# A Macaron block with one Strassen-Winograd level: the quads' merge regrouped, one output half accumulated upon a sum in PSUM

## The chip, the cores and the metric

One core of one Trainium2 chip runs the whole block. The metric is the device time of one execution in microseconds, as the median of several runs. The program is also run once under the hardware profiler, which gives each engine's instructions with their start and length.

## The reference

A Macaron block of width 2048 on 256 tokens: a SwiGLU feed-forward network (FFN) of inner width 5632, a mixer (an RWKV-7 branch and a pooling branch), and a second FFN. All inputs are float32.

```python
D_MODEL = 2048
SEQ = 256
D_FF = 5632

def _swiglu(x, w_gate, w_up, w_down):
    return (jax.nn.silu(x @ w_gate) * (x @ w_up)) @ w_down
...
        f = _swiglu(_rmsnorm(h, ln_ffn1_pre[l]), ffn1_gate[l], ffn1_up[l], ffn1_down[l])
        h = h + MACARON_WEIGHT * _rmsnorm(f, ln_ffn1_post[l])
...
        h = h + _rmsnorm(mx, ln_mix_post[l])
        f = _swiglu(_rmsnorm(h, ln_ffn2_pre[l]), ffn2_gate[l], ffn2_up[l], ffn2_down[l])
        h = h + MACARON_WEIGHT * _rmsnorm(f, ln_ffn2_post[l])
```

## The kernel before

**Products.** A float32 product is made of three matmuls (`mm3`, L317): each operand is split into a rounded high part and a low part, and high by high, high by low and low by high are added up in a PSUM bank. The low and high parts of a weight tile are made on the fly: ScalarE (ACT) casts the tile (`wH`), VectorE (DVE) subtracts the cast from the tile (`wL`, called a *low* here), TensorE (PE) multiplies. The pairs `wH`, `wL` lie in a ring of five buffers (`WS_BUFS`), so a cast waits until PE has used the tile five entries back.

**Blocks.** `seven` (L508) computes two output column blocks of 512 at once: `f` (first) and `l` (last), each for the two halves of the tokens (0 and 1), in four PSUM banks f0, f1, l0, l1. In an FFN's gate and up stage a block is 512 columns of gate (`f`) and the same of up (`l`), with 16 tiles of the inner dimension; there are blocks 0 to 10, and blocks 2 to 10 use this function with quads. Blocks 0 and 1 have none. In the down stage two calls make four column blocks of the output; the second has a *trail* of 16 inner tiles that are multiplied half by half after all else, the first half of the tokens first (`by_half`).

**Orders.** What PE does in a block is written out in a string. `f` or `l` is a *pair*: two inner tiles by one column block, both halves, 12 matmuls. `q` is a *quad*: two inner tiles by both column blocks and both halves, done with seven products in place of eight (one Strassen-Winograd level), 21 matmuls where two pairs take 24. A quad needs sums of the activations (`sums`), made once per stage, and sums of the weight tiles (t13, two halves of t24), made on DVE for every quad, as well as seven lows in four instructions. Four of its products go to banks of their own (p1, p5, p6, p7), the others into f0, l0 and l1.

**Merge.** After the last quad of a block, `merge` adds the four p banks up: ACT copies p1 into u0, then DVE makes u1 = p6 + u0, u2 = p7 + u1, u1 = p5 + u1, u3 = p5 + u2 (L645). DVE adds f0 to u1 and f1 to u3 when the pairs of `f` are done (also L645), and l0 to u0 and l1 to u2 when the block is done (`total`, L693). That is eight additions of 512 columns. ACT applies silu to the gate half, DVE multiplies (`mult`, L1074) and transposes in 32-by-32 blocks (`turn`, L875).

**What sets the order.** PE follows the strings. The order on DVE, ACT and the queues comes from a planner (`Plan.solve`) that gives each operation a due time, counted back from the PE step that needs it, and places the operations with fixed costs. It sets an order only: at run time each engine works through its list and waits on semaphores.

**Ends.** After the trail, `end` (L1185) squares the last column block, adds up, takes the power -1/2 on GpSimd (POOL), scales and writes out. In the FFNs the squares are summed by a DVE instruction (L1173); in the mixer's output stage, where `direct` is true, by ACT (L987).

Of the kernel before, what the change touches and what calls it, by code (L numbers as in the profile page):

```python
# [13 lines left out]
ALU = mybir.AluOpType  # L14
# [33 lines left out]
GATE_UP = ["", "ffffffffllllllll"] + ["ffqfqfqlqlll", "fffqffqlqllll", "ffqfqfqlqlll", "fffqffqlqllll", "ffqfqfqlqlll", "fffqffqlqllll", "ffqfqfqlqlll", "fffqffqlqllll", "ffqfqfqlqlll"]  # L48
# [172 lines left out]
class Block:  # L221
# [95 lines left out]
    def mm3(s, ps, aH, aL, bH, bL, start, stop):  # L317
        nc = s.nc
        nc.tensor.matmul(ps, aH, bH, start=start, stop=False)  # L319
        nc.tensor.matmul(ps, aH, bL, start=False, stop=False)  # L320
        nc.tensor.matmul(ps, aL, bH, start=False, stop=stop)  # L321
# [99 lines left out]
    def sums(s, T, Td, j, out, own=None, nq=2, used=(), x32=None):  # L421
# [13 lines left out]
        def second():  # L435
# [72 lines left out]
    def seven(s, wf, cf, wl, cl, at, dep, KT, need, sm, order, ev_f, ev_l, used, trail=0):  # L508
# [9 lines left out]
        left = dict(f0=std + n, f1=std, l0=std + n, l1=std + n, p1=n, p5=n, p6=n, p7=n)  # L518
# [9 lines left out]
        def mul(b, x, wt):  # L528
            left[b] -= 1
            new = b not in bank  # L530
            if new:
                bank[b] = s.psum("ms") if b[0] == "p" else s.pm.tile(
                    [P, 512], F32, tag="mm", name=s.nm("mm"))
            s.mm3(bank[b], *x, *wt, new, left[b] == 0)
# [9 lines left out]
        def pair(k, w, c0, b, by_dma):  # L544
            low, dst = s.fetch(w, k, c0, keep, by_dma, by_dma)

            def do():
                for i in range(2):
                    for h in range(2):
                        mul(f"{b}{h}", rows(k + i, h), ws[k + i])  # L550
            d = p.pe(12 * MM, do, [low, dep(k)] + claim(b + "0", b + "1"), dst)
# [3 lines left out]
        def quad(q):  # L555
# [10 lines left out]
            def get(m):  # L566
# [3 lines left out]
                w, c0 = ((wl, cl), (wf, cf))[(m + i) % 2]  # L570
# [32 lines left out]
            def half(n_, m, deps, rel):  # L603
# [15 lines left out]
                                  mul("f0", S_(4), x["a"][1])),  # L619
                 [la, ds, dep(k)] + claim("p1", "f0", "f1"), ra)  # L620
            p.pe(3 * MM, lambda: mul("l0", rows(k + 1, 0), x["b"][0]),
                 [lb] + claim("l0", "l1"), rb)
# [4 lines left out]
                                      mul("l1", rows(k + 1, 1), x["t24"][1])),  # L627
# [14 lines left out]
        def add(o, b, i):  # L642
            if u[o] is None:
                new(o)
            V.tensor_tensor(out=u[o], in0=bank[b], in1=u[i], op=ALU.add)  # L645
        m, use = {}, {}

        def merge(d):
            for i in range(4):
                use[i] = p.claim("tmp")  # L650
# [3 lines left out]
            for o, b, i in ((1, "p6", 0), (2, "p7", 1), (1, "p5", 1), (3, "p5", 2)):  # L654
                d = m[f"u{o}"] = p.op("DVE", one, lambda o=o, b=b, i=i: add(o, b, i),
                                      [d] + (use[o][0] if o > 1 or b == "p6" else []))
                held[b].append(d)
                use[i][1].append(d)
        nq, last = 0, {}
        ks = dict(f=iter(range(K0, KT, 2)), l=iter(range(K0, KT - trail, 2)))  # L660
        for c in order:
# [12 lines left out]
            if c == "f" and left["f"] == std // 2:  # L674
                m["f"] = last["f"]

                def close_f():
                    for h, i in ((0, 1), (1, 3)):
                        if n:
                            d = p.op("DVE", one, lambda h=h, i=i: add(i, f"f{h}", i),  # L680
                                     [last["f"], m[f"u{i}"], last["q"]])
# [5 lines left out]
                if not n or "u3" in m:  # L687
# [4 lines left out]
        def total(h):  # L692
            V.tensor_tensor(out=u[2 * h], in0=bank[f"l{h}"], in1=u[2 * h], op=ALU.add)  # L693
# [1321 lines left out]
```

## Time and profile before

| what | value |
|---|---|
| median of 3 runs | 2017.59 us (2016.92 to 2018.37) |
| the profiled execution's span | 2015.4 us |
| PE busy | 2000.9 us |
| DVE busy | 1824.7 us |
| ACT busy | 1192.3 us |
| granted TensorE clock, mean | 0.998 |

The profiled execution has no time of its own beside the span, which runs from its first to its last instruction; the timed runs contain about 2.2 us more (2017.59 less 2015.4), the start and the end around it. Busy shares over the whole span mix stages: the mixer lies between about 700 and 1340 us, the first FFN before and the second behind it.

### The profile page before, as it was taken

Reading aid. Unit: us, or ns where it says so; the run is one execution under the profiler, and the core shown is the slowest. Engines: PE = TensorE matmul, PEld = TensorE weight load, DVE = VectorE, ACT = ScalarE, POOL = GpSimd, SP = SyncE. Lnnn points to the kernel's source line nnn. Section 1 sums busy time; section 2 is a strip of 40 time slices with the busy share of each in tenths; the row PEclk is TensorE's granted clock in tenths of the full one; section 3 lists DMA queues with packets and bytes.
Section 4 is the critical chain, followed back from the end, with each engine's and each line's share of the span. In section 5 each row is a group of like instructions: output and inputs, shape, how many; then the busy total and the mean of one; then the engine's idle time right before and its main releaser. Section 6 shows DMA issues by size and latency. Waiting matters only on the chain.

```text
span 2015.4 us, 28684 instructions
## 1 busy us (share of the span) xinstructions
PE 2000.9 (99%) x9957; PEld 1655.1 (82%) x9957; DVE 1824.7 (91%) x2424; ACT 1192.3 (59%) x1586; POOL 327.6 (16%) x673
## 2 busy tenths in 40 slices
PE   9999999999999999999999999999999999999997
PEld 7888888888888888888788788888888888888886
DVE  6999999999999957789689678979999999999997
ACT  7555665556666566685476434665656555566663
POOL 0111211131000123403220111011113111310000
PEclk9999999999999999999999999999999999999999
DMA  7675674667568577757456547666656747665683
GB/s 268 224 241 182 220 242 160 218 213 241 175 203 299 209 212 214 205 175 214 146 173 190 159 168 269 244 216 215 228 198 218 245 142 235 211 228 183 207 294 126
DMA packets 227419, 423.56 MB, mean 210 GB/s; under 512 B 24639, under 2 KB 28105, under 8 KB 227273
## 3 DMA queue, kind: packets, MB, share of 16 engines
q1 hardware_dynamic: 204713, 384.70, 57.9%
q0 software_dynamic: 22272, 36.51, 5.5%
q8 instruction: 78, 1.28, 0.3%
q10 hardware_dynamic: 288, 0.52, 0.1%
q14 instruction: 68, 0.56, 0.1%
HBM read 396.69 MB, written 8.39 MB: 201 GB/s over the span
## 4 chain that ended last, share of the span: by engine, by line
PE 97%; DVE 1%; issue 1%; DMA 0%; ACT 0%; POOLq 0%; POOL 0%; DVEq 0%; ACTq 0%
PE mm L319 27%; PE mm L321 26%; PE mm L320 26%; PE ms L320 5%; PE ms L321 5%; PE ms L319 5%; PE tr L849 1%; PE pA L1733 0%; DVE u L645 0%; PE mc L817 0%; DMA x<-in_x_dram 0%; PE pU L1829 0%; PE pSa L1841 0%; PE pY L1864 0%; PE pT L1900 0%
## 5 line engine op out<-in xcount | busy, mean ns | idle before, releaser
L319 PE MATMUL mm<-wH,xH 128*128 128x512 f32 (+1 forms) x2116 | 825.5, 391 | 0.0
L320 PE MATMUL mm<-wL,xH 128*128 128x512 f32 (+1 forms) x2116 | 821.2, 388 | 0.0
L321 PE MATMUL mm<-wH,xL 128*128 128x512 f32 (+1 forms) x2116 | 821.1, 388 | 0.0
L319 PEld LDWEIGHTS mm<-wH,xH 128*128 128x128 f32 x2116 | 397.4, 188 | 82.1
L321 PEld LDWEIGHTS mm<-wH,xL 128*128 128x128 f32 x2116 | 397.4, 188 | 82.0 <-DVE xL L867 0.2
L373 ACT CAST wH<-w 128x1024 fp32r<-128x1024 f32 x313 | 326.2, 1054 | 231.7 <-PE mm L321 208.1
L320 PEld LDWEIGHTS mm<-wL,xH 128*128 128x128 f32 x2116 | 397.7, 188 | 79.7
L383 DVE TENSOR_TENSOR wL<-w,wH 128x1024 fp32r<-128x1024 f32 x313 | 373.0, 1218 | 18.9 <-ACT wH L373 17.3
L593 ACT CAST wH<-t 128x1024 fp32r<-128x1024 f32 x208 | 219.4, 1055 | 217.0 <-PE mm L321 108.9
L296 DVE TENSOR_TENSOR wL<-w,wH 128x1024 fp32r<-128x1024 f32 (+2 forms) x200 | 236.6, 1192 | 95.7 <-ACT wH L295 94.1
L295 ACT CAST wH<-w 128x1024 fp32r<-128x1024 f32 (+2 forms) x200 | 205.4, 1034 | 170.9 <-PE mm L321 150.7
L892 POOL DMA_DIRECT2D x<-T x352 | 173.1, 499 | 729.8 <-DVE T L875 190.3
L598 DVE TENSOR_TENSOR wL<-t,wH 128x1024 fp32r<-128x1024 f32 x208 | 248.6, 1217 | 0.7 <-ACT wH L593 0.7
L593 ACT CAST wH<-w 128x1024 fp32r<-128x1024 f32 x208 | 168.3, 835 | 56.6 <-PE mm L321 30.0
L598 DVE TENSOR_TENSOR wL<-w,wH 128x1024 fp32r<-128x1024 f32 x208 | 194.5, 951 | 0.3
L576 DVE TENSOR_TENSOR t<-w,w 128x1024 f32<-128x1024 f32 x104 | 126.7, 1218 | 0.0
L320 PE MATMUL ms<-wL,sH 128*128 128x512 f32 x276 | 107.6, 390 | 0.2
L319 PE MATMUL ms<-wH,sH 128*128 128x512 f32 x276 | 107.4, 389 | 0.0
L321 PE MATMUL ms<-wH,sL 128*128 128x512 f32 x276 | 107.4, 389 | 0.0
L585 DVE TENSOR_TENSOR t<-w,t 128x512 f32<-128x512 f32 x104 | 71.8, 690 | 2.6
L581 DVE TENSOR_TENSOR t<-w,t 128x512 f32<-128x512 f32 x104 | 71.3, 686 | 0.6
L645 DVE TENSOR_TENSOR u<-ms,u 128x512 f32<-128x512 f32 x92 | 61.4, 686 | 1.4
(317 smaller groups left out, 2107.8 us busy)
## 6 DMA issues: line engine op xcount, KB each, us to landing
w<-in_w_in_dram SPq DMA_DIRECT2D x128, 512.0 KB
w<-in_ffn_up_dram SPq DMA_DIRECT2D x112, 512.0 KB
w<-in_ffn_gate_dram SPq DMA_DIRECT2D x110, 512.0 KB
w<-in_ffn_down_dram SPq DMA_DIRECT2D x104, 512.0 KB
w<-in_ffn_down_dram SPq DMA_DIRECT2D x144, 256.0 KB
w<-in_ffn_gate_dram SPq DMA_DIRECT2D x132, 256.0 KB
w<-in_ffn_up_dram SPq DMA_DIRECT2D x128, 256.0 KB
w<-in_w_out_dram SPq DMA_DIRECT2D x24, 512.0 KB
```

Source lines behind the costliest of these rows:

```text
L295: s.nc.scalar.copy(vH, v)
L296: s.nc.vector.tensor_tensor(out=vL, in0=v, in1=vH.bitcast(F32), op=ALU.subtract)
L319: nc.tensor.matmul(ps, aH, bH, start=start, stop=False)
L320: nc.tensor.matmul(ps, aH, bL, start=False, stop=False)
L321: nc.tensor.matmul(ps, aL, bH, start=False, stop=stop)
L373: nc.scalar.copy(x["H"], x["v"])
L383: nc.vector.tensor_tensor(out=x["L"], in0=x["v"], in1=x["H"].bitcast(F32), op=ALU.subtract)
L576: V.tensor_tensor(out=v["t13"], in0=v["a"], in1=v["b"][:, :1].to_broadcast([P, 2, 512]), op=ALU.subtract)
L585: V.tensor_tensor(out=v["t24"][:, 1], in0=v["b"][:, 1], in1=v["t24"][:, 0], op=ALU.subtract)
L593: nc.scalar.copy(H, src)
L598: V.tensor_tensor(out=L, in0=src, in1=H.bitcast(F32), op=ALU.subtract)
L892: nc.gpsimd.dma_start(out=x[0][q * 32:q * 32 + 32, i], in_=src[i * 32:i * 32 + 32, q])
```

## The change

- The signs of two sums of the activations are turned, so that two instructions of `sums` become plain additions and subtractions, and p5 is subtracted.
- In a quad the roles of the column blocks are exchanged: the fourth sum's product goes to l0, the two direct products to f0 and f1. l1 gets nothing from a quad.
- In a gate-up block, where all `l` pairs now come after the last quad (`early` is false), u2 - p5 is not kept in SBUF: DVE writes it into l1's PSUM bank (`seed`), and PE accumulates the `l` pairs on it (no start flag). The first `l` pair is cut in two: its half 0 needs only its weights, its half 1 also the seed. At the block's end there is one `total` (l0); l1 is multiplied and transposed from its bank. The merge has seven additions.
- In the down stage's second call (and only there) DVE adds u3 into l1 and u1 into l0 in their banks (`into`) before the trail; PE's first trail product needs both. No `total` follows the trail, and the last column block is read from PSUM; its squares are summed on ACT.
- Orders: gate-up blocks 2 to 10 had 4, 3, 4, 3, 4, 3, 4, 3, 4 quads (32) and have 4, 4, 3 three times over (33), in other places of the string. The down and output strings are the same.

```diff
-GATE_UP = ["", "ffffffffllllllll"] + ["ffqfqfqlqlll", "fffqffqlqllll", ...]
+Q4, Q3 = "ffqqfqqfllll", "fffqfqqflllll"
+GATE_UP = ["", "ffffffffllllllll"] + [Q4, Q4, Q3] * 3
...
-    def mm3(s, ps, aH, aL, bH, bL, start, stop):
+    def mm3(s, ps, aH, aL, bH, bL, start, stop, seeded=False):
...
-            V.scalar_tensor_tensor(out=f[:, 0], in0=a21, scalar=-1.0, in1=a22, op0=ALU.mult,
-                                   op1=ALU.subtract)
-            V.scalar_tensor_tensor(out=f[:, 1], in0=f[:, 0], scalar=-1.0, in1=a11,
-                                   op0=ALU.mult, op1=ALU.subtract)
+            V.tensor_tensor(out=f[:, 0], in0=a21, in1=a22, op=ALU.add)
+            V.tensor_tensor(out=f[:, 1], in0=f[:, 0], in1=a11, op=ALU.subtract)
...
-        left = dict(f0=std + n, f1=std, l0=std + n, l1=std + n, p1=n, p5=n, p6=n, p7=n)
+        left = dict(f0=std + n, f1=std + n, l0=std + n, l1=std, p1=n, p5=n, p6=n, p7=n)
+        early = "l" in order[:order.rfind("q") + 1].lower()
+        ready = []
+        cut = {}
+        if n and not early:
+            cut["l1"] = std
+        if n and early and trail:
+            cut["l1"] = std - 2 * order[:order.rfind("q")].count("l")
+        if n and trail:
+            cut["l0"] = std - 2 * order[:order.rfind("q")].count("l")
...
-            d = p.pe(12 * MM, do, [low, dep(k)] + claim(b + "0", b + "1"), dst)
+            deps = [low, dep(k)] + claim(b + "0", b + "1")
+            if b == "l" and ready:
+                p.pe(6 * MM, lambda: do((0,)), deps)
+                d = p.pe(6 * MM, lambda: do((1,)), ready, dst)
+            else:
+                d = p.pe(12 * MM, lambda: do((0, 1)), deps, dst)
...
-                w, c0 = ((wl, cl), (wf, cf))[(m + i) % 2]
+                w, c0 = ((wf, cf), (wl, cl))[(m + i) % 2]
...
-                                  mul("f0", S_(4), x["a"][1])),
+                                  mul("l0", S_(4), x["a"][1])),
...
-            p.pe(3 * MM, lambda: mul("l0", rows(k + 1, 0), x["b"][0]),
+            p.pe(3 * MM, lambda: mul("f0", rows(k + 1, 0), x["b"][0]), [lb], rb)
...
-                                      mul("l1", rows(k + 1, 1), x["t24"][1])),
+                                      mul("f1", rows(k + 1, 1), x["t24"][1])),
...
+        def seed():
+            bank["l1"] = s.pm.tile([P, 512], F32, tag="mm", name=s.nm("mm"))
+            V.tensor_tensor(out=bank["l1"], in0=u[2], in1=bank["p5"], op=ALU.subtract)
+
+        def into(h, i):
+            V.tensor_tensor(out=bank[f"l{h}"], in0=bank[f"l{h}"], in1=u[i], op=ALU.add)
...
-            for o, b, i in ((1, "p6", 0), (2, "p7", 1), (1, "p5", 1), (3, "p5", 2)):
+            for o, b, i in ((1, "p6", 0), (2, "p7", 1), (3, "p5", 2), (1, "p5", 1)):
+                if o == 3 and not early:
+                    d = p.op("DVE", one, seed, [d])
+                    ready.append(d)
...
+            if early and trail:
+                d = p.op("DVE", one, lambda: into(1, 3), [m["u3"]])
+                ready.append(d)
+            if trail:
+                d = p.op("DVE", one, lambda: into(0, 1), [m["u1"]])
+                ready.append(d)
...
-                    for h, i in ((0, 1), (1, 3)):
+                    for h, i in ((0, 0), (1, 2)):
...
-            def finish(h, d):
-                d = p.op("DVE", one, lambda: total(h), [d, m["u0"], m["u3"]], due=p.clk)
-                ev_l(h, d, lambda: u[2 * h], None)
...
-                      keep, finish, [dep(k) for k in range(KT - trail, KT, 4)],
-                      used)
+                      keep, lambda h, d: ev_l(h, d, lambda: bank[f"l{h}"], held[f"l{h}"]),
+                      [dep(k) for k in range(KT - trail, KT, 4)] + ready, used)
...
-            if n:
-                d = p.op("DVE", one, lambda h=h: total(h), [p.last, m["u0"], m["u3"]])
+            i = 1 + 2 * h
+            if n and f"u{i}" in m:
+                d = p.op("DVE", one, lambda h=h, i=i: total(h, i), [p.last, m[f"u{i}"]])
...
-        part, direct = [None, None], KT == NKD
+        part, direct = [None, None], True
```

PE has six matmuls of 512 columns fewer (8,870 rows in its list for 8,876), DVE 12 instructions fewer of 2,426: 18 additions fewer, ten instructions more for the two quads less their four pairs, four fewer at the ends of the FFNs, SP four DMA issues more.

**DVE at the end of a four-quad block of the first FFN's gate-up stage**, from the lows of the last pairs through the merge (u are the sums in SBUF, ms the p banks, mm the f and l banks). Before:

```order
L383 TENSOR_TENSOR wL_2884<-w_601_2655,wH_2883 128x1024
L383 TENSOR_TENSOR wL_2899<-w_621_2722,wH_2898 128x1024
L383 TENSOR_TENSOR wL_2908<-w_634_2782,wH_2907 128x1024
L383 TENSOR_TENSOR wL_2922<-w_635_2784,wH_2921 128x1024
L645 TENSOR_TENSOR u_2953<-ms_2710,u_2942 128x512
L645 TENSOR_TENSOR u_2955<-ms_2702,u_2953 128x512
L645 TENSOR_TENSOR u_2953<-ms_2698,u_2953 128x512
L645 TENSOR_TENSOR u_2973<-ms_2698,u_2955 128x512
L645 TENSOR_TENSOR u_2953<-mm_2631,u_2953 128x512
L645 TENSOR_TENSOR u_2973<-mm_2635,u_2973 128x512
L383 TENSOR_TENSOR wL_2945<-w_638_2802,wH_2944 128x1024
L383 TENSOR_TENSOR wL_2971<-w_639_2804,wH_2970 128x1024
```

Now:

```order
L384 TENSOR_TENSOR wL_2492<-w_533_2343,wH_2491 128x1024
L384 TENSOR_TENSOR wL_2501<-w_535_2352,wH_2500 128x1024
L384 TENSOR_TENSOR wL_2510<-w_538_2362,wH_2509 128x1024
L384 TENSOR_TENSOR wL_2522<-w_546_2397,wH_2521 128x1024
L661 TENSOR_TENSOR u_2548<-ms_2345,u_2541 128x512
L661 TENSOR_TENSOR u_2553<-ms_2335,u_2548 128x512
L666 TENSOR_TENSOR mm_2556<-u_2553,ms_2331 128x512
L384 TENSOR_TENSOR wL_2544<-w_547_2399,wH_2543 128x1024
L659 TENSOR_TENSOR u_2548<-u_2548,ms_2331 128x512
L384 TENSOR_TENSOR wL_2565<-w_550_2410,wH_2564 128x1024
L661 TENSOR_TENSOR u_2541<-mm_2261,u_2541 128x512
L661 TENSOR_TENSOR u_2553<-mm_2265,u_2553 128x512
```

The four lows ahead of the merge belong to pairs in both; the third addition now writes an mm bank, which is l1, and a pair's low comes ahead of the second use of p5.

**DVE where one gate-up block ends and the next begins** (T is the block's gated product, transposed; t are sums of weight tiles of the next block's quads). Before:

```order
L693 TENSOR_TENSOR u_2942<-mm_2690,u_2942 128x512
L693 TENSOR_TENSOR u_2955<-mm_2714,u_2955 128x512
L598 TENSOR_TENSOR wL_3024<-w_649_2840,wH_3023 128x512
L598 TENSOR_TENSOR wL_3045<-t_680_3006,wH_3044 128x1024
L576 TENSOR_TENSOR t_689_3062<-w_659_2892,w_666_2925 128x1024
L581 TENSOR_TENSOR t_692_3067<-w_659_2892,t_689_3062 128x512
L598 TENSOR_TENSOR wL_3065<-t_685_3026,wH_3064 128x1024
L585 TENSOR_TENSOR t_692_3067<-w_666_2925,t_692_3067 128x512
```

Now:

```order
L729 TENSOR_TENSOR u_2548<-mm_2311,u_2548 128x512
L1108 TENSOR_TENSOR u_2548<-u_2548,u_2541 128x512
L1108 TENSOR_TENSOR mm_2556<-mm_2556,u_2553 128x512
L909 STREAM_TRANSPOSE T_605_2664<-u_2548 128x4x4x32
L909 STREAM_TRANSPOSE T_605_2664<-mm_2556 128x4x4x32
L612 TENSOR_TENSOR wL_2659<-t_593_2609,wH_2658 128x1024
L612 TENSOR_TENSOR wL_2679<-t_596_2614,wH_2678 128x1024
L599 TENSOR_TENSOR t_600_2642<-w_567_2482,t_600_2642 128x512
```

The products and transposes, which stood among the next block's lows, now follow the one total at once.

**DVE at the last quad of the second FFN's down stage**, from the low of its t24 (fg are the scaled outputs of the first two column blocks). Before:

```order
L598 TENSOR_TENSOR wL_18707<-t_3841_18688,wH_18706 128x1024
L1159 TENSOR_TENSOR fg_13143<-u_17940,gb_13141 128x512
L383 TENSOR_TENSOR wL_18718<-w_3794_18486,wH_18717 128x1024
L383 TENSOR_TENSOR wL_18725<-w_3807_18544,wH_18724 128x1024
L383 TENSOR_TENSOR wL_18735<-w_3808_18546,wH_18734 128x1024
L383 TENSOR_TENSOR wL_18745<-w_3809_18549,wH_18744 128x1024
L383 TENSOR_TENSOR wL_18761<-w_3810_18552,wH_18760 128x1024
L1159 TENSOR_TENSOR fg_13143<-u_17945,gb_13141 128x512
L1159 TENSOR_TENSOR fg_13145<-u_17948,gb_13141 128x512
L645 TENSOR_TENSOR u_18784<-ms_18043,u_18764 128x512
L383 TENSOR_TENSOR wL_18781<-w_3823_18618,wH_18780 128x1024
L645 TENSOR_TENSOR u_18796<-ms_18036,u_18784 128x512
```

Now:

```order
L384 TENSOR_TENSOR wL_18708<-w_3788_18477,wH_18707 128x1024
L384 TENSOR_TENSOR wL_18715<-w_3801_18535,wH_18714 128x1024
L1193 TENSOR_TENSOR fg_13139<-u_17935,gb_13137 128x512
L1193 TENSOR_TENSOR fg_13141<-u_17938,gb_13137 128x512
L1193 TENSOR_TENSOR fg_13141<-u_17940,gb_13137 128x512
L661 TENSOR_TENSOR u_18757<-ms_18035,u_18751 128x512
L661 TENSOR_TENSOR u_18759<-ms_18024,u_18757 128x512
L659 TENSOR_TENSOR u_18761<-u_18759,ms_18020 128x512
L659 TENSOR_TENSOR u_18757<-u_18757,ms_18020 128x512
L384 TENSOR_TENSOR wL_18725<-w_3802_18537,wH_18724 128x1024
L669 TENSOR_TENSOR mm_18071<-mm_18071,u_18761 128x512
L669 TENSOR_TENSOR mm_17999<-mm_17999,u_18757 128x512
```

Before them now stand the low of t24 and one product fg, as in the first row and the second before. The additions of the merge stand together, and the two `into` additions follow the low of the trail's first pair.

More of the change, by code (lines that the diff above doesn't have):

```diff
@@ L533, in mul @@
                     [P, 512], F32, tag="mm", name=s.nm("mm"))
-            s.mm3(bank[b], *x, *wt, new, left[b] == 0)
+            s.mm3(bank[b], *x, *wt, new, left[b] in (0, cut.get(b)),
+                  b in cut)
         def rows(k, h):
@@ L644, in add @@
                 new(o)
-            V.tensor_tensor(out=u[o], in0=bank[b], in1=u[i], op=ALU.add)
+            if b == "p5":
+                V.tensor_tensor(out=u[o], in0=u[i], in1=bank[b], op=ALU.subtract)
+            else:
+                V.tensor_tensor(out=u[o], in0=bank[b], in1=u[i], op=ALU.add)
         m, use = {}, {}
+        def seed():
[3 more added lines that the diff above has]
+            V.tensor_tensor(out=bank[f"l{h}"], in0=bank[f"l{h}"], in1=u[i], op=ALU.add)
         def merge(d):
-            for i in range(4):
+            for i in range(3 + early):
                 use[i] = p.claim("tmp")
```

32 lines of the change are left out of this document (17 added, 15 removed).

## The prediction

> **What bounds the kernel now.** First the page: engines, clock, and the chain of waits by engine.
>
> ```profile
> span 2015.4 us, 28684 instructions
> PE 2000.9 (99%) x9957; PEld 1655.1 (82%) x9957; DVE 1824.7 (91%) x2424; ACT 1192.3 (59%) x1586; POOL 327.6 (16%) x673
> PEclk9999999999999999999999999999999999999999
> PE 97%; DVE 1%; issue 1%; DMA 0%; ACT 0%; POOLq 0%; POOL 0%; DVEq 0%; ACTq 0%
> ```
>
> PE is never without work but for 14.5 us (2015.4 less 2000.9): some 3 at the start, 11 behind the last matmul. So nothing can be won beyond matmuls removed and the tail; what can be lost is PE waiting. Who is near to making it wait is read in the gate-up stage, block by block (windows from one block's L693 to the next; columns are the stretch, its length with DVE busy and instructions, clock, DMA).
>
> ```profile
> 140.88:182.71 41.83, 41.40 (x49) 1.00 0.68 224
> 182.71:224.97 42.26, 41.69 (x49) 1.00 0.61 203
> 390.88:429.17 38.29, 37.78 (x45) 1.00 0.63 211
> ```
>
> DVE is busy 99% of each. It has no time to spare either, yet PE does not stop: DVE is just in time. Its price list, from the groups of lines between 136 and 500 us and the timeline (start, length, repeats):
>
> ```profile
> L383 DVE TENSOR_TENSOR wL<-w,wH 128x1024 fp32r<-128x1024 f32 x82 | 97.5, 1217 | 1.7 <-ACT wH L373 1.3
> L875 DVE STREAM_TRANSPOSE T<-u 128x512 f32<-128x512 f32 x18 | 12.7, 707 | 0.2
> L1074 DVE TENSOR_TENSOR u<-u,u 128x512 f32<-128x512 f32 x18 | 12.2, 681 | 0.0
> L645 DVE TENSOR_TENSOR u<-mm,u 128x512 f32<-128x512 f32 x18 | 11.5, 682 | 0.0
> 297.76 2.73 DVE L645 TENSOR_TENSOR u<-ms,u 128x512 f32<-128x512 f32 x4
> 300.41 1.28 DVE L645 TENSOR_TENSOR u<-mm,u 128x512 f32<-128x512 f32 x2
> 1974.88 5.76 DVE L383 TENSOR_TENSOR wL<-w,wH 128x1024 fp32r<-128x1024 f32 x5
> ```
>
> An instruction overlaps the end of the one before. From start to start a 1024 column operation takes (5.76 - 1.22) / 4 = 1.135 us; a 512 column one 1.28 - 0.68 = 0.60 where the next does not need its result, and (2.73 - 0.68) / 3 = 0.68 on a mean where some do. I count 0.64 for each of 512, 0.68 for a transpose. The instructions of blocks 3, 4 and 9 in the order, so priced, are 41.6, 42.0 and 38.0 us; the windows above took 41.83, 42.26 and 38.29. The prices hold within 1%, small waits included.
>
> ```profile
> 99.26 0.39 PE L319 MATMUL mm<-wH,xH 128*128 128x512 f32 x1
> 140.06 0.39 PE L319 MATMUL mm<-wH,xH 128*128 128x512 f32 x1
> 100.87 1.40 DVE L1010 SCALAR_TENSOR_TENSOR sg<-mm,rs,sg 128x512 f32<-128x512 f32 x2
> 140.88 1.28 DVE L693 TENSOR_TENSOR u<-mm,u 128x512 f32<-128x512 f32 x2
> ```
>
> PE begins block 2 at 99.26 and block 3 at 140.06: 180 matmuls (four quads, eight pairs) in 40.80 us, 0.2267 each. A quad is 4.76 us, a pair 2.72. A four-quad block is 40.8, a three-quad one 41.5.
>
> **The change part by part.** *Matmuls.* One quad more in each FFN replaces two pairs: 2 x 3 matmuls, 6 x 0.2267 = 1.36 us less. Certain, as PE sets the time.
>
> *DVE's total.* Per FFN nine additions go (-5.8 us), one quad comes: t13 and three lows of 1024 columns, two halves of t24 and one low of 512, 4 x 1.135 + 3 x 0.64 = 6.5 us, less the lows of two pairs, 2.3. Net -1.6 us of about 370: no relief to speak of, and none that PE could use, since PE already runs through. The two turned instructions in `sums` are of 256 columns and few; nothing.
>
> *The seed, a new wait on PE.* In a four-quad block the half 1 of the first `l` pair comes 4 quads, 4 `f` pairs and half a pair after PE's block start: 138 matmuls, 31.28 us (three quads: 129, 29.24). DVE must by then have done everything from the last block's `total` through the seed. In the order for block 6 this is 18 operations of 1024, 14 of 512 and two transposes: 30.75 us. So DVE may begin `total` 0.48 us after PE begins the block (0.05 for the signal), or PE waits. All blocks so, first the time from total to seed (S), then from seed to next total (R), counted in the order:
>
> block 3: S 30.75, R 11.14; block 4 (three quads): 28.05, 14.30; 5: 30.11, 11.29; 6: 30.75, 10.61; 7 (three): 28.59, 12.43; 8: 30.75, 10.65; 9: 30.25, 9.87.
>
> Where does DVE stand? Its product at 100.87 has one 0.62 us operation less ahead of it now: 100.25. To block 2's seed are 29.58, done at 129.83; PE wants it at 99.26 + 31.28 = 130.54: no wait. To `total` 11.29 more, 141.12, 1.05 after 140.06. From here: wait = lateness + S + 0.05 - 31.28 (or 29.24); next lateness = R - 0.05 less what PE has left from the seed (9.52 us; 12.24 in a three-quad block) if PE waited. Block 3: 0.57, then late 1.57. Block 4: 0.43, late 2.01. Block 5: 0.89, late 1.72. Block 6: 1.24, late 1.04. Block 7: 0.44, late 0.14. Blocks 8 to 10: none. Sum 3.6 us per FFN. Behind the waiting matmul stand all of PE's; DVE loses nothing by it. Before, `l` pairs stood between the last quads, and no PE step waited for the merge. With prices 1% lower (DVE's 0.4 to 0.6 us idle per block used up) the sum is 1.5; 1% higher, about 6. I take 3.0, nearer the counted value: 6.0 for both FFNs.
>
> The Trainium skill, *Perfetto Trace Analysis*, Optimizing Scalar/DVE Operations, gives DVE about 60 ns of access overhead per instruction on SBUF and 125 on PSUM. Seed, product and transpose of l1 now touch PSUM more than before; by that rule up to 0.2 us more per block, 2 us in the ten blocks that wait. Here an addition from PSUM (682 ns, L645) took as long as a product in SBUF (681, L1074), so the sum leaves it out; a write to PSUM no row here shows.
>
> *The trail, a second new wait.* Around the down stage's last quad before, DVE and PE:
>
> ```profile
> 1972.01 2.35 DVE L598 TENSOR_TENSOR wL<-t,wH 128x1024 fp32r<-128x1024 f32 x2
> 1974.28 0.68 DVE L1159 TENSOR_TENSOR fg<-u,gb 128x512 f32<-128x512 f32 x1
> 1981.77 0.68 DVE L645 TENSOR_TENSOR u<-ms,u 128x512 f32<-128x512 f32 x1
> 1975.78 0.39 PE L319 MATMUL ms<-wH,sH 128*128 128x512 f32 x1
> 1982.58 0.39 PE L319 MATMUL mm<-wH,xH 128*128 128x512 f32 x1
> 1893.24:1973.15 79.91, 79.56 (x90) 1.00 0.70 243
> ```
>
> The low of t24 starts at 1973.15 (2.35 less 1.22 after 1972.01) and PE uses it at 1975.78; the trail starts at 1982.58. The merge began at 1981.77 and nobody waited for it. From the totals to this low DVE had 79.9 us by the count and 79.91 by the window; now the same but for two halves of t24 that moved behind the totals. So the low starts where it did. From there to the second `into`: 1.135 (low), 0.64 (fg), 2 x 1.135 (lows of f), 3 x 0.64 (fg), 2.7 (four additions, chained), 1.135 (low), 1.33 (two `into`): 11.13, done at 1984.28 and wanted at 1982.58. PE waits 1.7 us in each FFN, 3.4 in all; with the three fg done earlier in DVE's slack 0, if the merge slips as it did before up to 5. The lows behind it take 1.135 each against PE's 1.36 per step: the delay ends there.
>
> *The end.* Rows of the last matmul and the chain behind it; then the mixer's end, which has ACT's path already.
>
> ```profile
> 2004.12 0.39 PE L321 MATMUL mm<-kH,xL 128*128 128x512 f32 x1
> 2004.54 0.69 DVE L693 TENSOR_TENSOR u<-mm,u 128x512 f32<-128x512 f32 x1 [5.59 <-PE mm L321]
> 2005.27 0.75 DVE L1173 CUSTOM_DVE_ANT_0 junk<-u,rp 128x512 bf16<-128x512 f32 x1
> 2006.12 0.92 POOL L1178 TENSOR_TENSOR rs<-rt,mhalf 128x1 f32<-128x1 f32 x1 [9.94 <-DVE rt L1173]
> 1318.04 0.60 ACT L987 ACTIVATE junk<-mm 128x512 bf16<-128x512 f32 x1 [0.26 <-PE mm L321]
> 1318.54 0.20 ACT L987 ACTIVATION_READ_ACCUMULATOR junk<-mm 128x1 f32 x1
> 1319.71 0.20 DVE L1170 TENSOR_SCALAR rt<-ss,rp 128x1 f32<-128x1 f32 x1
> ```
>
> From PE's end (2004.51) to POOL: 1.61 us before. Now ACT from 2004.55, 0.70 to its sum's end (1318.04 to 1318.74), a hop of 0.1, DVE 0.20, a hop of 0.1: 1.14. Gain 0.5 us at the kernel's end (0.3 to 0.7); at the first FFN's end PE has other work.
>
> *The sum*: -1.36 - 0.5 + 6.0 + 3.4 = +7.5 us. The span goes from 2015.4 to 2022.9; the runs shown lie 2.2 above the span, so the median goes from 2017.6 to 2025.1.
>
> **The rivals.** *No new wait* (the other side): PE keeps running since DVE's waits for ACT, 0.4 to 0.6 us in a block, shrink when DVE is late, and the merge comes in time. For it: the total work of DVE falls. Against: S leaves 0.5 us in 31. It decides itself at a lateness under 0.5 us in every block. Time: 2017.6 - 1.9 = 2015.7.
>
> *The trail alone waits*: 2015.7 + 3.4 = 2019.1. For it: the gate-up count stands on 1% of 31 us, the trail's on 1.7 of 11.
>
> *DVE paces the gate-up stage*: writes into PSUM and chained additions cost more than counted. The chain p6, p7, seed runs at 0.72, not 0.60: a block's lateness grows by 0.3 to 0.5 and blocks 8 and 9 wait too; 6 us or more per FFN, and 5 in the two trails: 2015.7 + 12 + 5 = 2033. The Trainium skill, *VectorE: DVE Perf Modes*, The DRAIN you can't avoid, has it that a semaphore between chained operations costs nothing; by that rule the chain would run at the unchained pace and this rival lose its ground. This trace differs: four chained additions took 2.73 us, where four at 0.60 would take 2.48.
>
> *The added quads do not lighten PE*: the order's list shows six matmuls fewer, so this is out.
>
> **How the numbers follow.** Forecast (waits in both places, 2021.7 to 2030): 0.5. Trail alone: 0.14. No new wait: 0.16. DVE paces: 0.16. Other, among it a gain of more than 4 us, for which PE has nearly no idle time: 0.04. 0.2% is 4 us, about what a measurement of this kernel can tell from no change. Faster by more (under 2013.6): 0.03. Within: 0.32, from the trail alone, no wait and a little of the forecast's lower edge. Slower: 0.65. The forecast alone spans 2021 to 2030; the range for 8 in 10 takes in the case without waits at 2015.5 and most of the worst at 2032.
>
> **What would show it.** PE's row of waits gains entries on DVE: on the seed (PE mm after DVE mm, ten or so, 0.4 to 1.3 us each) and on `into` (two, 1.7 us each). PE's busy time falls by 1.4 us while its idle grows by about 9. DVE's seeds end 0.05 us before the first accumulating matmul of l1 in blocks 3 to 7. From last matmul to POOL's power 1.1 us. If PE shows no waits in the gate-up stage, the lateness was over-counted, and the time is 2019 or less.

## The result, and the profile after

| | before | after |
|---|---|---|
| median, 5 runs each | 2016.96 us (2016.92 to 2018.37) | 2024.05 us (2023.68 to 2024.95) |
| ratio | | 1.0035, 95% interval [1.0023, 1.0047] |
| span of the profiled execution | 2015.4 us | 2022.0 us |

The change makes the kernel 7 us slower. The page of the changed kernel first (busy times, then the shares of the chain that ended last):

```profile
span 2022.0 us, 28723 instructions
PE 2003.0 (99%) x9951; PEld 1652.3 (82%) x9951; DVE 1820.4 (90%) x2412; ACT 1200.5 (59%) x1598; POOL 325.7 (16%) x673
PE 67%; DVE 19%; DMA 8%; issue 5%; SPq 1%; ACT 0%; POOL 0%; DVEq 0%; POOLq 0%
```

Six matmuls fewer, as the order had it, and DVE 4 us less busy; yet the chain now leads through DVE for 19% where it was 1%. PE's waits (total, times, longest) say at which instructions it meets DVE; neither of these two rows stood there before:

```profile
PE mm L320 <- DVE mm L669: 2.9, 2, 1.4
PE mm L320 <- DVE mm L666: 2.3, 6, 0.7
```

L666 is the seed, L669 is `into`. The timeline (start, length, and in brackets the idle time before) of PE at the seeds of blocks 3 and 6, and of DVE at that of block 3:

```profile
170.71 0.39 PE L322 MATMUL mm<-wH,xL 128*128 128x512 f32 x1
171.36 0.49 PE L320 MATMUL mm<-wH,xH 128*128 128x512 f32 x1 [0.27 <-DVE mm L666]
171.69 0.39 PE L321 MATMUL mm<-wL,xH 128*128 128x512 f32 x1
...
296.07 0.50 PE L320 MATMUL mm<-wH,xH 128*128 128x512 f32 x1 [0.70 <-DVE mm L666]
```

```profile
166.90 2.35 DVE L384 TENSOR_TENSOR wL<-w,wH 128x1024 fp32r<-128x1024 f32 x2
169.17 1.41 DVE L661 TENSOR_TENSOR u<-ms,u 128x512 f32<-128x512 f32 x2
170.61 0.70 DVE L666 TENSOR_TENSOR mm<-u,ms 128x512 f32<-128x512 f32 x1
```

The seed ends at 171.31 and the matmul starts 0.05 later. From start to start PE took 0.65 us where its pitch is 0.2267, so the stop cost 0.43, not the 0.27 in brackets (the matmul before is recorded until 171.10), and the next step took 0.33, another 0.10. All costs of waits below are such sums: start to start, less 0.2267. So counted, gate-up blocks 3, 5, 6 and 8 lose 0.54, 0.46, 0.97 and 0.17 us in the first FFN; the three-quad blocks 4 and 7 lose under 0.1 each. As a whole, from the first matmul of block 2 to the first behind block 10, the stage takes 371.79 us in place of 369.92 with three matmuls (0.68 us) fewer: 2.55 us lost, and 2.57 in the second FFN (371.81). Before, it ran at the pitch without loss.

The view that shows this without the trace's single rows is the number of matmuls that fit into a fixed stretch of the first gate-up stage (windows; length, PE, PEld, DVE, ACT, POOL busy, clock, DMA). Before, then after:

```profile
99.30:473.00 373.70, 373.70 (x1650) 309.46 (x1649) 369.10 (x421) 224.05 (x251) 70.72 (x144) 1.00 0.64 213
```

```profile
99.30:473.00 373.70, 372.55 (x1639) 306.86 (x1638) 367.12 (x416) 225.35 (x251) 70.36 (x144) 1.00 0.64 216
```

Eleven matmuls fewer got done in the same 373.7 us: 11 x 0.2267 = 2.5 us lost. DVE is busy 99% of it before and 98% after.

The trail, first FFN, on DVE and then on PE:

```profile
665.89 2.35 DVE L612 TENSOR_TENSOR wL<-t,wH 128x1024 fp32r<-128x1024 f32 x2
...
672.85 1.41 DVE L661 TENSOR_TENSOR u<-ms,u 128x512 f32<-128x512 f32 x2
674.29 1.29 DVE L659 TENSOR_TENSOR u<-u,ms 128x512 f32<-128x512 f32 x2
675.49 1.22 DVE L384 TENSOR_TENSOR wL<-w,wH 128x1024 fp32r<-128x1024 f32 x1
676.63 1.29 DVE L669 TENSOR_TENSOR mm<-mm,u 128x512 f32<-128x512 f32 x2
```

```profile
678.07 0.47 PE L320 MATMUL mm<-wH,xH 128*128 128x512 f32 x1 [1.45 <-DVE mm L669]
```

From the second low's start (665.89 + 2.35 - 1.22 = 667.02) to the end of the second `into` (677.92) DVE took 10.90 us; PE waits 1.61 us and loses 0.08 on the next step, 1.7 per FFN.

The end of the kernel:

```profile
2010.82 0.39 PE L322 MATMUL mm<-kH,xL 128*128 128x512 f32 x1
2011.25 0.69 DVE L1193 TENSOR_TENSOR fg<-mm,gb 128x512 f32<-128x512 f32 x1 [5.80 <-PE mm L322]
2012.03 0.60 ACT L1021 ACTIVATE junk<-mm 128x512 bf16<-128x512 f32 x1 [10.25 <-DVE fg L1193]
2012.53 0.19 ACT L1021 ACTIVATION_READ_ACCUMULATOR junk<-mm 128x1 f32 x1
2012.75 0.21 DVE L1204 TENSOR_SCALAR rt<-ss,rp 128x1 f32<-128x1 f32 x1 [0.81 <-ACT junk L1021]
2013.06 0.54 POOL L1212 TENSOR_TENSOR rs<-rt,mhalf 128x1 f32<-128x1 f32 x1 [10.38 <-DVE rt L1204]
```

ACT did not start its squares when the last matmul was done (2011.21) but at 2012.03, behind DVE's product of the same bank: the bracket names it. POOL starts 1.85 us after PE's end, not 1.61 as before, and its power takes 0.54 us in place of 0.92.

The books: lost in gate-up 2.55 + 2.57, in the trails 2 x 1.69, matmuls -1.36: 7.1 us. PE's last matmul ends at 2011.21 in place of 2004.51, 6.70 later, since PE began block 2 0.40 sooner (98.86 for 99.26) and took 0.1 less for the mixer. The sooner start is not shown to be the change's: before, PE waited 1.2 us for the first DMA of x, and in the kernels below block 2 begins anywhere between 98.8 and 100.3. Behind the last matmul lie 10.79 us, before 10.89. The span grew by 6.6.

### The profile page after: what moved, and what is told of

Read it like the earlier page. It is cut to its first block, busy times and chain, and to the rows that moved or that the text cites. A ratio compares the mean times of both kernels' runs of the same rounds, so it can differ in the third digit from the quotient of the medians.

```text
span 2022.0 us, 28723 instructions
## 1 busy us (share of the span) xinstructions
PE 2003.0 (99%) x9951; PEld 1652.3 (82%) x9951; DVE 1820.4 (90%) x2412; ACT 1200.5 (59%) x1598; POOL 325.7 (16%) x673
## 4 chain that ended last, share of the span: by engine, by line
PE 67%; DVE 19%; DMA 8%; issue 5%; SPq 1%; ACT 0%; POOL 0%; DVEq 0%; POOLq 0%
PE mm L320 19%; PE mm L322 19%; PE mm L321 19%; DVE wL L612 6%; DVE wL L384 4%; DMA w<-in_ffn_down_dram 3%; DMA w<-in_ffn_gate_dram 3%; PE ms L320 2%; PE ms L321 2%; PE ms L322 2%; DVE t L590 2%; DMA w<-in_ffn_up_dram 2%; DVE u L661 1%; DVE t L595 1%; DVE t L599 1%
## 5 line engine op out<-in xcount | busy, mean ns | idle before, releaser
L607 ACT CAST wH<-t 128x1024 fp32r<-128x1024 f32 x212 | 223.6, 1055 | 197.1 <-PE mm L322 96.8
L321 PEld LDWEIGHTS ms<-wL,sH 128*128 128x128 f32 x282 | 52.9, 188 | 12.2 <-DVE wL L612 1.1
```

The costliest lines, as they stand in the source:

```text
L321: nc.tensor.matmul(ps, aH, bL, start=False, stop=False, skip_group_check=seeded)
L607: nc.scalar.copy(H, src)
```

## The experiments

Twelve kernels in three groups. Ratios are to the kernel before, which ran beside each of them with a median of 2016.9 to 2017.0 us.

### First: the two waits, each taken away

**a_old_orders**: the old gate-up strings.

```diff
-GATE_UP = ["", "ffffffffllllllll"] + [Q4, Q4, Q3] * 3
+GATE_UP = ["", "ffffffffllllllll"] + ["ffqfqfqlqlll", "fffqffqlqllll", "ffqfqfqlqlll", "fffqffqlqllll", "ffqfqfqlqlll", "fffqffqlqllll", "ffqfqfqlqlll", "fffqffqlqllll", "ffqfqfqlqlll"]
```

> The changed kernel, but the gate-up stage keeps its old strings (l pairs stand between the last quads, 32 quads per FFN), so that no seed is written there and a total stands at each block's end again; the down stage keeps both accumulations upon l's banks. Theory (PE's waits on the seed are 2.1 us per FFN, those on the down stage's trail 1.7): no wait of PE on a seed, 12 matmuls more, i.e. 2024.0 - 4.2 + 1.4 = 2021.2 us; the two trail waits of 1.6 to 1.7 us remain. Rival 1 (the extra quads make VectorE the pace, the seed only shows it): about the same, 2021, but then the run with the seed covered does not get faster. Rival 2 (the loss is in the start, the end or the rewritten additions, not in the waits): 2025.

Measured: 2020.18 us, 1.0019 [1.0011, 1.0028]. No seed wait, and the gate-up stage has 0.26 us of stops as before the change; the trails keep theirs (2.8 us in two waits by the profile). The gate-up part of the change costs 2024.05 - 2020.18 = 3.9 us net.

**b_no_into**: the totals behind the trail again.

```diff
-            if early and trail:
-                d = p.op("DVE", one, lambda: into(1, 3), [m["u3"]])
-                ready.append(d)
-                use[3][1].append(d)
-            if trail:
-                d = p.op("DVE", one, lambda: into(0, 1), [m["u1"]])
-                ready.append(d)
-                use[1][1].append(d)
...
+            def finish(h, d):
+                i = 1 + 2 * h
+                d = p.op("DVE", one, lambda: total(h, i), [d, m[f"u{i}"]], due=p.clk)
+                use[i][1].append(d)
+                ev_l(h, d, lambda: u[i], None)
...
```

> The changed kernel, but in the down stage's last call the totals u1 + l0 and u3 + l1 are formed behind the trail, as before the change; the gate-up stage with its seeds and 33 quads stays. Theory: the two trail waits vanish, 3.4 us: 2024.0 - 3.4 = 2020.6, or up to 0.5 more because the kernel's end has one addition behind the last matmul again. Rival 2 (the waits are covered by something else that ends as late): 2024. The seed's waits in the gate-up stage stay as they are, about 2.1 us per FFN.

Measured: 2024.28, 1.0036 [1.0023, 1.0049]: no gain. The time is rival 2's, but nothing else in the trail ended as late: its waits are gone, and PE has three new rows of waits elsewhere, in the mixer between the FFNs:

```profile
PE pA L1759 <- DVE R L1735: 1.3, 2, 1.1
PE pB L1778 <- DVE R L1770: 1.1, 2, 0.8
PE mm L320 <- ACT sgb L1395: 0.6, 1, 0.6
```

Nothing of the mixer was edited. But the instructions of DVE and ACT there stand in another order in this kernel, while before, after and a_old_orders share one where these waits lie. The kernel g_both below settles it.

**c_cover**: one `f` pair behind the last quad.

```diff
-Q4, Q3 = "ffqqfqqfllll", "fffqfqqflllll"
+Q4, Q3 = "fqqfqqffllll", "ffqfqqfflllll"
```

> The changed kernel with the same counts of quads and pairs, but in each gate-up block one f pair moved from ahead of the quads to behind the last one, so that PE has 12 matmuls (2.72 us) more between the last quad and the seeded bank, and the order puts one low of 1024 columns (1.135 us) behind the seed that stood ahead of it. Theory (a seed is late by 0.1 to 1.0 us because VectorE's lows for later pairs stand ahead of the merge, while those pairs are wanted later): all seed waits vanish, 2024.0 - 4.2 = 2019.8. Rival 1 (VectorE is short of time over whole blocks, so that the wait only moves): PE waits for the lows of l pairs or for quads instead, 2023 or more.

Measured: 2033.14, 1.0079 [1.0065, 1.0093]. No wait on a seed is left, and the kernel is 9 us slower than the changed one. Of this 3.6 belong to the mixer's other order, which this kernel has too, and 2.1 are one wait of PE on ACT's cast of a tile (kH) in the second FFN's trail, whose cause is not shown. In its first gate-up stage PE waits for the lows of quads in place of the seed:

```profile
99.30:473.00 373.70, 372.23 (x1631) 304.95 (x1630) 366.53 (x416) 226.14 (x250) 70.37 (x144) 1.00 0.63 213
```

```profile
PE ms L321 <- DVE wL L612: 1.3, 4, 0.4
```

19 matmuls missing, 4.3 us, where the changed kernel loses 2.5. So the seed's wait can be covered, but it only moves to other work of DVE, as rival 1 has it; the theory that covering the seed wins its time back falls.

**d_split**: each half of the trail waits for its own accumulation.

```diff
-            for o, b, i in ((1, "p6", 0), (2, "p7", 1), (3, "p5", 2), (1, "p5", 1)):
+            steps = [(1, "p6", 0), (2, "p7", 1), (3, "p5", 2), (1, "p5", 1)]
+            if trail:
+                steps[2:] = steps[:1:-1]
+            for o, b, i in steps:
...
+                if trail and b == "p5":
+                    d = p.op("DVE", one, lambda o=o: into(o // 2, o), [d])
+                    ready.append(d)
...
-                         [low, *deps, *at],
+                         [low, *deps, *at, *per[h]],
...
-                      [dep(k) for k in range(KT - trail, KT, 4)] + ready, used)
+                      [dep(k) for k in range(KT - trail, KT, 4)], used,
+                      per=(ready[:1], ready[1:]))
```

> The changed kernel, but in the down stage's last call p5 goes to u1 first, the accumulation upon l0 follows at once, that upon l1 later, and each half of the trail waits for its own accumulation alone. Theory (the wait is the count of work ahead of the second accumulation: 11.1 us where PE gives 9.4): l0's accumulation comes 9.2 us after the low of t24 starts, just in time, and l1's is wanted 10.9 us later still: both trail waits fall from 1.7 to under 0.3, 2024.0 - 3 = 2021.0. Rival (the wait moves to the second half, since l1's accumulation now stands behind seven lows): 0.5 to 1.5 us of wait there, 2022 to 2023.

Measured: 2025.18, 1.004 [1.0027, 1.0052]. Of the trail waits 0.4 us is left in the first FFN and nothing in the second, and no wait of the second halves; the mixer has the other order and the same three waits as in b_no_into, which eat the gain.

### Second: is it the seed, or VectorE's time?

**h_old_split**: the strings of a_old_orders with the split of d_split; its mixer has the order of before.

> The old gate-up strings (no seed, 32 quads) together with the split accumulation of the down stage's trail (u1 and l0 first, each half waiting for its own). The order of the mixer's instructions between the two FFNs is here the same as before the change; in the kernels without the accumulation upon l, with the f pair moved, and with the split alone it was another. Theory (those three lost 3.5 us in the mixer because of that other order, which hid what their edits gained): no wait on a seed, at most 0.4 us on the accumulation in each FFN, none of the mixer's waits: 2020.2 - 3.0 = 2017.2. Rival (the mixer waits because the first FFN's end comes sooner, whatever the order): 2020.5.

Measured: 2016.64, 0.9999 [0.999, 1.0008], span 2014.9. No PE wait in gate-up or trails, and in the mixer only the one of 0.3 us that was there before. Against a_old_orders the split is worth 3.5 us, the whole of the trail's loss. DVE in the second FFN's trail, where l0's `into` (L670) comes alone and ends at 1981.96:

```profile
1979.10 1.41 DVE L662 TENSOR_TENSOR u<-ms,u 128x512 f32<-128x512 f32 x2
1980.54 0.69 DVE L660 TENSOR_TENSOR u<-u,ms 128x512 f32<-128x512 f32 x1
1981.26 0.70 DVE L670 TENSOR_TENSOR mm<-mm,u 128x512 f32<-128x512 f32 x1
1981.87 4.62 DVE L384 TENSOR_TENSOR wL<-w,wH 128x1024 fp32r<-128x1024 f32 x4
```

**o_reorder**: lows of later `l` pairs put behind the seed, on DVE alone.

```diff
...
+        for first, seed, lows in s.moves:
+            at = order.index(first)
+            back = [n for n in order[:at] if n in lows]
+            for n in back:
+                order.remove(n)
+            at = order.index(seed) + 1
+            order[at:at] = back
...
```

> The changed kernel, all counts and strings kept; in the order, those lows of the second and later l pairs that stood ahead of a gate-up block's merge (two of 1.135 us in blocks 3 and 6) are put behind the seed. The mixer's order is unchanged. Theory (PE waits because VectorE works ahead on pairs wanted 2.7 us later): the seed waits of 0.05 to 1.0 us vanish or fall under 0.2, 2024.0 - 3.8 = 2020.2. Rival 1 (VectorE is short of time over whole blocks): PE waits for l pairs' lows in place of the seed, 2022.5 to 2024.

Measured: 2034.1, 1.0084 [1.007, 1.0098], the worst of all. The matmuls of the first gate-up stage, PE's waits there, DVE around the seed of block 6, and DVE's own waits ahead of a merge:

```profile
99.30:473.00 373.70, 370.48 (x1618) 302.10 (x1617) 364.16 (x413) 221.30 (x246) 70.38 (x144) 1.00 0.63 211
```

```profile
PE ms L329 <- DVE wL L622: 2.0, 4, 1.0
PE mm L329 <- DVE wL L392: 1.0, 1, 1.0
```

```profile
293.89 2.35 DVE L392 TENSOR_TENSOR wL<-w,wH 128x1024 fp32r<-128x1024 f32 x2
297.09 1.42 DVE L671 TENSOR_TENSOR u<-ms,u 128x512 f32<-128x512 f32 x2 [0.85 <-ACT u L663]
```

```profile
DVE u L671 <- ACT u L663: 4.7, 5, 1.4
```

With nothing to do ahead of the merge, DVE stands waiting for the last quad and ACT's copy of p1, 0.85 us in block 6 and 4.7 us in five blocks. The changed kernel has no such wait. PE is 32 matmuls short, 7.3 us: 4.8 more than the changed kernel loses, nearly what DVE stood idle. The lows ahead of the merge were what DVE filled this time with. Both theories put the time too low; rival 1's mechanism is what the rows show.

**f_alt**: 32 quads with the new kind of string.

```diff
-GATE_UP = ["", "ffffffffllllllll"] + [Q4, Q4, Q3] * 3
+GATE_UP = ["", "ffffffffllllllll"] + [Q4, Q3] * 4 + [Q4]
```

> The changed kernel with four-quad and three-quad blocks in turn (32 quads per FFN, the seeds stay, 12 matmuls more). Theory as counted (a four-quad block's seed waits even behind a three-quad block, as block 5 did with 0.46 us): waits of 0.3 to 0.5 us in some four-quad blocks, about 1 us per FFN; 2024.0 + 1.4 - 2.2 = 2023.2. Rival 1 (the 33rd quad alone overloads VectorE): no seed wait is left, 2021.2.

Measured: 2023.47, 1.0031 [1.0019, 1.0044], near the theory's sum, though not by its account: only some of the stops are at a seed, others at lows of quads. Against a_old_orders, which has the same 32 quads, this is 3.3 us more: the strings cost it, not the 33rd quad.

**p_33_inter**: 33 quads, `l` pairs between them, the split, and s_best's end (below).

```diff
-GATE_UP = ["", "ffffffffllllllll"] + [Q4, Q4, Q3] * 3
+GATE_UP = ["", "ffffffffllllllll"] + ["ffqfqfqlqlll", "fffqffqlqllll", "ffqfqfqlqlll"] * 3
```

> 33 quads per FFN, but l pairs between the last quads as before the change and totals at the blocks' ends (no seed), the split accumulation upon l in the trail, and at the kernel's end the product behind ScalarE's squares on the same bank. Theory (VectorE can carry 33 quads where no PE step waits on the merge): 12 matmuls less than before (-1.4), -0.7 at the end, up to 0.8 of wait in the trails: 2017.0 - 1.5 = 2015.5. Rival 1 (33 quads are too much for VectorE): PE waits for lows, 2 us or more, 2018 or later.

Measured: 2022.15, 1.0024 [1.0014, 1.0033]: the theory misses by 6.6 us. The gate-up stage loses 8 matmuls (x1642), 1.8 us, on lows, and the down stage waits too (0.9 to 1.2 us on a low and 0.7 at the trail in each FFN): VectorE does not carry the 33rd quad in these strings even without any seed.

### Third: the deciding kernels

**t_no_seed**: the changed kernel's strings, but u3 kept as a sum.

```diff
-        early = "l" in order[:order.rfind("q") + 1].lower()
+        early = True
```

> The changed kernel with its strings and its 33 quads, but nothing is written into l's bank ahead of the pairs: u3 is formed as a sum of its own and added to l1 at the block's end, one addition more per block on VectorE. If it is the seed as a point where PE and VectorE must meet that costs the time, PE's gate-up waits vanish: 2024.0 - 4.2 = 2019.8. If VectorE is short of time over whole blocks (what the two kernels with moved work pointed to), the waits come back on the lows of quads or pairs, 2 us or more per FFN: 2024 to 2026.

Measured: 2029.81, 1.0062 [1.0049, 1.0074]. Nothing in PE's gate-up work waits for a merge here, but DVE has one addition more per block. PE loses more than with the seed, on lows of quads:

```profile
99.30:473.00 373.70, 371.16 (x1625) 303.79 (x1624) 368.97 (x423) 223.87 (x249) 70.52 (x144) 1.00 0.64 211
```

```profile
PE mm L321 <- DVE wL L612: 1.4, 2, 1.1
PE ms L321 <- DVE wL L612: 1.1, 5, 0.4
```

25 matmuls short, 5.7 us.

**r_lighter**: the product of half 1 left out in nine blocks of each FFN.

```diff
                 def mult():
+                    if h:
+                        return
```

> The changed kernel with every order kept, but the product of half 1's two outputs (512 columns, 0.60 to 0.68 us of VectorE) is left out in nine gate-up blocks of each FFN, so the output is not the reference's. If VectorE's time is what is short, 0.6 us less per block takes away most of the seed waits, which add up over blocks (0.54, 0.46, 0.97 and 0.17 now): 0.3 to 0.6 us per FFN are left, 2024.0 - 3.2 = 2020.8. If a seed's wait is a fixed price of the meeting (the write into PSUM, the signal), it stays, 2023.5 or more.

Measured: 2019.62, 1.0011 [1.0002, 1.002]. Seed and strings are as in the changed kernel, DVE has one 512 column operation less per block, and the seed's row is gone from PE's waits:

```profile
99.30:473.00 373.70, 373.70 (x1649) 308.97 (x1648) 365.31 (x412) 227.22 (x252) 70.36 (x144) 1.00 0.64 216
```

One matmul short; by the stage's length 0.4 us is lost in place of 2.55. The meeting of PE and DVE at the seed costs next to nothing once DVE has the time.

**g_both**: the edits of a_old_orders and b_no_into together.

> Both parts undone: the old gate-up strings, and the totals behind the trail as before the change; the rewritten additions, the turned subtractions and the end through ScalarE stay. PE should then wait neither on a seed nor on an accumulation. The order of the mixer's instructions is the other one here. Theory (the other order costs 3.5 us in the mixer by itself): 2016.7 + 3.5 = 2020.2, with waits of PE on R and sgb in the mixer. Rival (the mixer's waits in the three earlier kernels came from the gate-up or trail edits): 2016.8.

Measured: 2020.84, 1.002 [1.0011, 1.0029]. Neither seed nor accumulation is waited for. The three waits in the mixer are there, and its order is the other one, as the theory had it; h_old_split, with the order of before, takes 4.2 us less. DVE there, g_both and then the changed kernel:

```profile
891.80 1.23 DVE L297 TENSOR_TENSOR wL<-w,wH 128x1024 fp32r<-128x1024 f32 x1
892.94 0.48 DVE L1589 SCALAR_TENSOR_TENSOR yb<-mc,cols,yb 128x256 fp32r<-128x256 f32 x1
893.34 1.39 DVE L1735 TENSOR_TENSOR R<-R,R 64x512 f32<-64x512 f32 x2
```

```profile
892.16 0.68 DVE L1743 TENSOR_TENSOR R<-R,R 64x512 f32<-64x512 f32 x1
892.77 0.47 DVE L1597 SCALAR_TENSOR_TENSOR yb<-mc,cols,yb 128x256 fp32r<-128x256 f32 x1
893.16 1.21 DVE L297 TENSOR_TENSOR wL<-w,wH 128x1024 fp32r<-128x1024 f32 x1
```

A low stands ahead of the recurrence's first product (R) instead of behind it, and PE waits up to 1.1 us for R. The order of this stage is not in the strings; it changed with the first FFN's end in b_no_into, d_split and g_both and with the gate-up strings in c_cover. All four have the waits; of the kernels with the order of before none has. From the first FFN's trail to the trail of the mixer's output stage (first product with a kH tile in each) PE takes 622.8 us in these four and 619.1 to 619.2 in the kernel before and all others: the other order costs 3.6 us.

**s_best**: h_old_split, and at the end ACT's squares first, DVE's product behind them.

```diff
-            m = p.op("DVE", cost("DVE", 512), lambda: scale(h, 3, ap()), [d], due=t + 1)
+            m = p.op("DVE", cost("DVE", 512), lambda: scale(h, 3, ap()),
+                     [d, n0] if direct else [d], due=t + 1)
```

> The old gate-up strings, the split accumulation in the trail and, at the end, the product of the last bank placed behind ScalarE's squares of the same bank (they ran one behind the other, the product first). Theory (ScalarE waited 0.8 us for the product): from the last matmul's end to POOL's power 1.1 us in place of 1.85, the output 0.7 us sooner: 2016.6 - 0.7 = 2015.9, and a span of 2014.2. If the two do not wait for each other, nothing: 2016.6.

Measured: 2016.05, 0.9995 [0.9986, 1.0004], span 2014.1.

```profile
2003.66 0.39 PE L322 MATMUL mm<-kH,xL 128*128 128x512 f32 x1
```

```profile
2004.15 0.60 ACT L1022 ACTIVATE junk<-mm 128x512 bf16<-128x512 f32 x1 [9.88 <-PE mm L322]
...
2004.87 0.21 DVE L1205 TENSOR_SCALAR rt<-ss,rp 128x1 f32<-128x1 f32 x1 [6.70 <-ACT junk L1022]
...
2005.17 0.54 POOL L1213 TENSOR_TENSOR rs<-rt,mhalf 128x1 f32<-128x1 f32 x1 [9.78 <-DVE rt L1205]
```

ACT is released by PE, and POOL starts 1.12 us after PE's end (2004.05). This is the fastest of all kernels, 0.9 us under the one before and 8 under the changed one; against the one before that is no measured difference.

## Why the prediction was right, and where it was not

**The total.** +7.5 us forecast on the span, +6.6 measured; 2025.1 against 2024.05, where 0.6 of the difference is the base (2016.96 in five runs, 2017.59 in three). The waits stand at the two places the forecast named, and no rival's time was nearer. That the sum is so close is in part luck: the seeds cost 0.9 less than forecast, the end gained 0.4 less, and 0.5 came off at the start and in the mixer, which the sum did not have.

**Matmuls, -1.36 us.** x9957 to x9951 at an unchanged pitch: right.

**The trail, 3.4 us.** Right: 1.7 per FFN, from a count of 11.13 us of DVE's work that took 10.90; the 0.2 less was made up by 0.15 from the end of the second `into` to the matmul and 0.08 on PE's next step, which the count did not have. That this is all of it h_old_split shows: with the split, 3.5 us come back.

**The seed, 6.0 us.** Mis-sized: 5.1 us were lost in the two stages. The count had waits in blocks 3 to 7 of 0.57, 0.43, 0.89, 1.24 and 0.44; they were 0.54, 0.09, 0.46, 0.97, under 0.1, and 0.17 in block 8. The count had DVE's stretches a little too long. From total to seed, blocks 3 to 6 took 30.63, 27.90, 30.03 and 30.63 us where it had 30.75, 28.05, 30.11 and 30.75; from seed to next total 10.99, 13.99, 11.17 and 10.45 where it had 11.14, 14.30, 11.29 and 10.61. So each block carried on 0.2 to 0.5 us less lateness, the most in the three-quad block 4. The 1% in the prices that the forecast named as its uncertainty covers it.

**What the wait means.** The forecast was made by counting DVE's work against PE's, and that was sound. Its reading, a new wait because PE now meets the merge while "no PE step waited for the merge" before, was not. Where no seed is waited for, the first gate-up stage loses more and not less: 4.4 us in c_cover and 5.7 in t_no_seed, against 2.55. Where DVE stands idle ahead of the merge (o_reorder) it loses 7.4, and with 0.6 us less of DVE's work per block and the meeting kept (r_lighter) 0.4. The cause is the rival's, DVE as the pace of the gate-up stage, at the forecast's price and not at the rival's 2033. One gap stays: c_cover has another order and t_no_seed one addition more per block, and a kernel without the meeting but with the same work in the same order was not run. The rival's own reason, dearer writes into PSUM and chains, fails: a chained addition did take 0.72 us from start to start, but DVE's stretches took less than the count with its 0.64 had, and blocks 9 and 10 do not wait.

What the new strings do can be worked out from the forecast's prices: a quad takes 6.5 us of DVE for 4.76 of PE, a pair 1.1 for 2.72. "ffqqfqqf" wants 4 x 6.5 + 4 x 1.135 = 30.5 us of DVE in 29.9 of PE, before any merge; the light `l` pairs all come behind. Matmuls missing in the first gate-up stage, in us, for the kernels in turn: 32 quads with `l` between them 0 (a_old_orders), 33 quads so 1.8 (p_33_inter), 33 in the new strings with the seed 2.5, without it 5.7. Both the place of the light pairs (f_alt against a_old_orders) and the 33rd quad cost, and in these strings the addition that the seed saves is worth more than its wait. "No relief to speak of" was right; "none that PE could use" held for the strings before, and r_lighter shows that with the new ones PE can use it. The sum had the bunching only as DVE's way to the seed; that it costs without a seed as well was not in it.

**The end, -0.5 us.** It gave 0.1, and that only because POOL's power was shorter. The step that failed is "ACT from 2004.55": the product of the last bank came first and ACT waited 0.8 us for it. With the order turned, s_best took 1.12 us from matmul to POOL, where the sum had 1.14.

**The two rules.** By the Trainium skill, *Perfetto Trace Analysis*, Optimizing Scalar/DVE Operations, an operation that touches PSUM would pay about 65 ns more than one on SBUF (125 for 60). The trace does not agree: the seed, from SBUF and PSUM into PSUM, took 696 ns on a mean, the product in SBUF 693, and a subtraction from PSUM 680.

```profile
L666 DVE TENSOR_TENSOR mm<-u,ms 128x512 f32<-128x512 f32 x9 | 6.3, 696 | 0.3
L1108 DVE TENSOR_TENSOR u<-u,u 128x512 f32<-128x512 f32 x9 | 6.2, 693 | 0.3
L659 DVE TENSOR_TENSOR u<-u,ms 128x512 f32<-128x512 f32 x9 | 6.1, 680 | 0.0
```

By the Trainium skill, *VectorE: DVE Perf Modes*, The DRAIN you can't avoid, a semaphore behind each operation costs nothing extra, measured there on copies. Here a chain costs 0.12 us per link: two chained additions and the seed start 1.44 us apart (169.17 to 170.61), the two unchained ones at 674.29 start 0.60 apart (1.29 less 0.69).

**What was to show it.** The rows on L666 and L669 came, six and two waits. That PE's busy time falls by 1.4 us while its idle grows by about 9 did not come: busy rose by 2.1 and idle by 4.5 (2022.0 - 2003.0 against 14.5), since a matmul is recorded 0.39 us long or more at a pitch of 0.2267, which hides the first 0.16 us of each stop and the slower step behind it.

## What to carry to other kernels

Where an engine is 98% busy behind the one that sets the time, price every step of a hand-written order in both engines' time and put the light steps between the heavy ones; a wait at a named instruction may only be where such a debt shows, and moving that instruction moves the wait. When a wait disappears in an experiment and the time does not, compare the order and the waits of stages that were not edited: here 3 to 4 us came and went with the order of another stage. Where an accumulation must come before a tail of products, give each half of the tail its own dependency, and put the operation that the chain waits for first on a shared bank.

## What the runs showed of the hardware that was not expected

A stop of PE costs more than the wait: the step after the first matmul took 0.33 to 0.35 us in place of 0.2267 at each seed (171.36 to 171.69), 0.1 us per stop, and 0.30 at `into`.
